# An encoder block on one core: output projection as seven products of halves, block sums by adding transfers, convolution norm inside attention, rows turned once

## The chip, the cores and the metric

The kernel runs on one core of one Trainium2 chip. The time is in device microseconds (us), one launch of the whole block. The engines of a core are TensorE (PE), VectorE (DVE), ScalarE (ACT), GpSimd (POOL) and SyncE (SP, which here only issues transfers); 16 DMA engines move data. Three runs of the kernel before gave 1063.12 to 1064.12 us, median 1063.84.

## The reference

One layer with 1024 tokens of width 1024, all in float32:

```python
h = rms_norm(x, norm1_g)
a, gate, q, k, v = jnp.split(h @ w_in, splits, axis=-1)
conv_out = conformer_conv(a, gate, dw_kernel, dw_bias, ln_g, ln_b)   # 512 channels
attn_out = neighbourhood_attention(norm(q), norm(k), v, rpb)         # 8 heads of 64
mix = jnp.concatenate([conv_out, attn_out], axis=-1)
x = x + mix @ w_out                                  # 1024 x 1024
h = rms_norm(x, norm2_g)
x = x + (silu(h @ w_gate) * (h @ w_up)) @ w_down     # width 2816
```

The convolution runs over positions with 31 taps per channel, then a LayerNorm over the 512 channels and a swish. Attention is over windows of 8 x 16 on a grid of 16 rows and 64 columns.

## The kernel before, in words

The whole block is one program in an order written out by hand; each engine works its list from front to back, and waits are put in where data or a buffer is needed. Matrix products use a split: each float32 operand is cut into a high part (a copy by ACT) and a low part (a subtraction by DVE or POOL), function `split`, lines 103 to 108, and one product becomes three matmuls, high x high, high x low, low x high (`mac`, lines 110 to 114). A matmul is 128x512. `weave` (line 119) puts a piece of other work between two groups of three matmuls.

Buffers come from pools with fixed counts: 22 tiles `G` of 128x1024, 6 tiles `H` of 128x4096, 3 raw tiles `R` for loads. In PSUM there are four banks `mm`, two `tp`, and a double one `cv`. Weights come through a list of loads (`want`); `take` (line 144) splits the next one and issues a load further ahead, so a load waits until the raw tile is free that an earlier split has read.

In order of time:

- Input projections: tiles of q, k, v (`nat`) and the gated convolution input (`glu_step`), with the convolution taps beside them on DVE (line 319), and some on ACT and POOL (lines 344, 345), summed into `u` at line 324.
- Attention (the loop at line 789), 32 pieces of two heads: `score_mm` (line 615), scores plus bias and exponential (lines 628, 630), normalisation on POOL (line 637), six transposes (line 646) with their copies (line 651), and the product with the values (line 662). Every fourth piece an output block is copied and split (lines 669, 674).
- Convolution norm after attention: the 512 channels of each of eight token tiles are turned to rows (line 728), statistics (lines 735, 736), root on ACT, scaling (lines 752, 756), then turned back and passed through the swish (lines 761, 762, 764).
- Output projection (`proj`, line 720): for each of eight token tiles and two halves of the columns, eight slices of the inner dimension, three matmuls each. Results are added to x from PSUM (`resid`, line 775). Weights `wo` are split by POOL.
- `norm2` (line 856) stores x for later, squares and sums on ACT; `norm2_out` (line 863) scales rows.
- FFN up: gate and up projections together as 2x2 blocks, in seven products per block i of 128 columns (m1 to m7, `product`, line 1013; `evac`, line 1024), 22 blocks. The weight operands are raw blocks or sums of them (`t_sums`, line 886, on DVE), split by `prep` (line 902). The token operands are A11, A12 (lines 991 to 995: four token tiles turned per slice) and S1, S2, S3, S4, A22, sums of halves of the normalised rows (`s_sum`, line 936), which `s_T` (line 950) turns and splits one after the other while the first products run.
- FFN down: seven products again (`down`, line 1211).

Of the kernel before, what the change touches and what calls it, by code (L numbers as in the profile page):

```python
# [7 lines left out]
F32R = mybir.dt.float32r  # L8
AF = mybir.ActivationFunctionType
# [3 lines left out]
P = 128  # L13
# [17 lines left out]
def layout(v):  # L31
# [4 lines left out]
    gu = np.stack([f["w_gate"], f["w_up"]]).reshape(2, KB, P, FB, P).transpose(3, 0, 2, 1, 4)  # L36
    wd = f["w_down"].reshape(FB, P, D)
# [14 lines left out]
        "wo": f["w_out"],  # L52
# [15 lines left out]
def build(ctx, tc, a):  # L68
# [22 lines left out]
    def SM(name, n=8):  # L91
        return T("sm", [P, 8], 16, name)[:, :n]

# [62 lines left out]
    def take_parts(jobs, n=4, sub=pool):  # L156
        i = pos[1]
        hi, lo = chunks[i][2]()
        w = 1024 // n

        def part(o):
            sl = slice(o, o + w)
            split(hi[:, sl], lo[:, sl], raws[i][:, sl], (sub,))
            if o + w == 1024:
                raws.pop(i)
                issue()
        pos[1] += 1
        jobs.extend(lambda o=o: part(o) for o in range(0, 1024, w))
# [18 lines left out]
    wo, woq = {}, {}  # L187

    def wo_dst(d, k0):
        def dst():  # L190
            if (d, k0 // 4) not in woq:
                woq[d, k0 // 4] = H(f"wo{d}{k0}", F32R)
            q = woq[d, k0 // 4]
            o = k0 % 4 * 1024
            hl = (q[:, o:o + 1024], q[:, o + 1024:o + 2048])
            for j in range(2):
                wo[d, k0 + j] = [w[:, j * 512:(j + 1) * 512] for w in hl]
            return hl
        return dst

    for d in range(2):
        for k0 in (4, 6, 0, 2):
            want(a["wo"][k0 * P:(k0 + 2) * P, d * 512:(d + 1) * 512].rearrange("(k p) m -> p k m", p=P),
                 f"wo{d}{k0}", wo_dst(d, k0), (pool,) * 4 if d == 0 and k0 < 4 else (pool,))
# [361 lines left out]
    for c in range(1, 4):  # L566
        for h in range(2):
            accs = {}
            for part in range(2):
                glu_step(c, h, part, accs)  # L570
                if c < 3 and part == 0 or c == 3 and (h, part) != (1, 1):
                    take(2 if c == 3 and h == part == 0 else 1)
    for t in range(8):
        project(0, t, head_post)
        if t % 2 == 0:
            take()
# [87 lines left out]

    def evac_hi(s_):
        rh, cb = order[s_]
        if rh == 0:
            at[cb] = [G(f"at{cb}{w}", F32R).rearrange("p (c t q) -> p c t q", c=4, t=2) for w in range(2)]
        act.copy(at[cb][0][:, :, rh], os_[s_])

    def evac_lo(s_, cs=slice(0, 4)):
        rh, cb = order[s_]
        hi, lo = [w[:, cs, rh] for w in at[cb]]
        dve.tensor_tensor(lo, os_[s_][:, cs], hi.bitcast(F32), OP.subtract)

    def value(t):
        z = nat(2, t)
# [35 lines left out]
    cm, x2, xn = [], {}, {}  # L713

    def lhs(k, t):
        if k < 4:
            return [w[:, k, t * P:(t + 1) * P] for w in cm]
        return [w[:, k - 4, t // 4, :] for w in at[t % 4]]

    def proj(t, d, acc, ks):  # L720
        for k in ks:
            mac(acc, lhs(k, t), wo[d, k], k == 4, k == 3)
            weave()

    def conv_T(t):
        y = cv(f"y{t}")[:, :512] if t in (0, 3) else tp(f"y{t}")
# [4 lines left out]
    cs = {}  # L731

    def conv_stats(t, y):
        st6, mv, sd = SM(f"bs{t}", 6), SM(f"bm{t}", 2), SM(f"bd{t}", 1)
        dve.bn_stats(st6, y)
        dve.bn_aggr(mv, st6)
        act.activation(sd, mv[:, 1:2], AF.Sqrt, bias=eps)
        cs[t] = y, mv, sd
        if 1 <= t <= 4:
            conv_scale(t - 1)  # L740
        if t >= 4:
            conv_scale(t)

    def conv_scale(t):
        y, mv, sd = cs.pop(t)
        r = SM(f"br{t}", 1)
        dve.reciprocal(r, sd)
        if t % 2 == 0:
            xx = G(f"xh{t}")
            xh.extend([xx[:, :512], xx[:, 512:]])  # L750
        if t >= 6:
            dve.tensor_scalar(xh[t], y, mv[:, 0:1], r, op0=OP.subtract, op1=OP.mult)
        else:
            nb = SM(f"bb{t}", 1)
            dve.scalar_tensor_tensor(nb, mv[:, 0:1], -1.0, r, OP.mult, OP.mult)
            act.activation(xh[t], y, AF.Identity, bias=nb, scale=r)

    def conv_silu(h, c):
        y = tp(f"z{h}{c}")
# [3 lines left out]
        hi, lo = [w[:, c, h * 512:(h + 1) * 512].rearrange("p (b i j) -> p i b j", b=4, j=16) for w in cm]  # L763
        split(hi, lo, y.rearrange("p (i b j) -> p i b j", b=4, j=16), (dve,))
# [9 lines left out]
    def resid(t, d, acc):  # L774
        dve.tensor_tensor(x2[t][:, d * 512:(d + 1) * 512], acc, x2[t][:, d * 512:(d + 1) * 512], OP.add)

    acc0, xh = [], []

    def attn_half(t):
        acc0.append(mm(f"pj{t}"))  # L780
        proj(t, 0, acc0[t], range(4, 8))

    def fill(*ks):
        if not acc0:
            act.activation(warm, eps, AF.Sqrt)
            acc0.append(mm("pj0"))
        proj(0, 0, acc0[0], ks)

    for i in range(2, 32 + 2):
# [6 lines left out]
        if i in (14, 22):  # L796
            take_parts(jobs)
        if i < 32:
            ss = score_mm(i)
        if i >= 32:  # L800
            fill(*((4, 5) if i == 32 else (6,)))
# [6 lines left out]
        flip_out(i - 2, 0)  # L808
        if i > 2:
# [3 lines left out]
            elif i > 6 and i % 4 in (0, 3):  # L813
                evac_lo((i + 1) // 4 - 2, slice(0, 2) if i % 4 == 3 else slice(2, 4))
        if jobs and i % 4 < 2:
            jobs.pop(0)()
    fill(7)

    cm += [H(f"cm{w}", F32R).rearrange("p (k s) -> p k s", s=S) for w in range(2)]
    conv_stats(0, conv_T(0))  # L820
    woven.extend([lambda: (weigh(31), evac_hi(7), evac_lo(7)), lambda: conv_stats(1, conv_T(1)), lambda: None])
    for t in range(2, 8):
        woven.extend([lambda t=t: conv_stats(t, conv_T(t)), lambda: None])
    take()
    attn_half(1)
    take()
    attn_half(2)
    attn_half(3)
    cc = cv("pj45")
    acc0 += [cc[:, :512], cc[:, 512:]]  # L830
    proj(4, 0, acc0[4], range(4, 8))
    act.activation(warm, eps, AF.Silu)
    conv_silu(0, 0)
    proj(5, 0, acc0[5], range(4, 8))
    for t in range(6):
        load_x2(t)
    later = [(0, c) for c in range(1, 4)] + [(1, c) for c in range(4)]
    woven.extend(lambda q=q: conv_silu(*q) for q in later)
    for ts in (range(4), (4, 5)):
        for k in range(4):  # L840
            for t in ts:
                mac(acc0[t], lhs(k, t), wo[0, k], False, k == 3)
                if t % 2:
                    weave()
        for t in ts:
            resid(t, 0, acc0[t])
    for t in range(6, 8):
        load_x2(t)
        acc0.append(mm(f"pj{t}"))
        proj(t, 0, acc0[t], (4, 5, 6, 7, 0, 1, 2, 3))  # L850
        take(2)
        resid(t, 0, acc0[t])
# [15 lines left out]

    HK, QF = KB // 2, FB // 2
    raw_gu, top, tsum = {}, {}, {}

    def load_gu(i, j):
        if i < FB:
            raw_gu[i, j] = R(f"gu{i}{j}")  # L880
            nc.sync.dma_start(raw_gu[i, j], a["gu"][ms[i], j])

    def lr(w):
        return w[:, :512], w[:, 512:]

    def t_sums(i, ns):
        (b11, b21), (b12, b22) = lr(raw_gu[i, 0]), lr(raw_gu[i, 1])
        for n in ns:
            if n in (1, 3):
                tsum[i, n // 2] = G(f"ts{i}{n}")  # L890
            o = lr(tsum[i, (n - 1) // 2])[(n - 1) % 2]
            l, r = ((b12, b11), (b22, lr(tsum[i, 0])[0]), (b22, b12), (b21, lr(tsum[i, 0])[1]))[n - 1]
            dve.tensor_tensor(o, l, r, OP.subtract)  # L893
# [3 lines left out]
    ms = [m + h * QF for m in range(QF) for h in range(2)]  # L897
    products = [(i, p) for p in ("m1", "m2", "m6", "m5", "m7", "m4", "m3") for i in range(2)]
    products += [(i, p) for i in range(2, FB) for p in ORDER]
    tasks = list(products)  # L900

    def prep(n=1):
        for _ in range(n):
# [3 lines left out]
            if i < 2:  # L907
                if i == 1 and p in ("m6", "m5"):
                    t_sums(i, (1, 2) if p == "m6" else (3, 4))
            elif p == "m1":  # L910
                t_sums(i, (1, 2))
            elif p == "m6":
                t_sums(i, (3, 4))
            b = {"m1": (0, 0), "m2": (0, 1), "m3": (1, 1)}.get(p)
            n = {"m5": 0, "m6": 1, "m7": 2, "m4": 3}.get(p)
            src = lr(raw_gu[i, b[0]])[b[1]] if b else lr(tsum[i, n // 2])[n % 2]
            top[i, p] = lr(G(f"t{i}{p}", F32R))
            split(*top[i, p], src, (dve,) if i < 2 and p in ("m1", "m2", "m6", "m5") else (pool,))
            if (i, p) == (0, "m2"):
                load_gu(1, 1)  # L920
            if (i, p) == (1, "m5"):
                load_gu(2, 0)
            if (i, p) == (0, "m3"):
# [330 lines left out]
```

## Time and profile before

| | |
|---|---|
| median of three runs | 1063.84 us |
| profiled execution | 1064.03 us, span 1062.2 us |
| instructions | 13969 |
| DVE busy | 699.8 us (66%) |
| ACT busy | 443.7 us (42%) |
| POOL busy | 397.3 us (37%) |
| moved by DMA | 144.05 MB, mean 136 GB/s |
| granted PE clock | 0.999 |

The span is the time from the first to the last instruction of one profiled execution; the rest of its own time lies around it. Busy time of an engine is the sum of its instructions. A group row reads: line, engine, operation, what is written <- what is read, shape, count | busy time, mean ns of one | idle time of the engine before them and what ended it. L112 is line 112. A chain row reads: start, length, what ran. PEld is the weight load of PE, which runs beside the matmuls.

### The profile page before, as it was taken

What the parts mean: (1) busy time and instruction counts of PE and PEld (TensorE: products, weight loads), DVE (VectorE), ACT (ScalarE), POOL (GpSimd) and SP (SyncE); (2) the same over time, 40 slices, a digit from 0 to 9 for tenths busy, and PEclk for the clock granted to TensorE, in tenths of its full rate; (3) what the DMA queues carried; (4) which work ended last, traced back from release to release, by engine and by line L of the source; (5) the groups of instructions that cost most, each with busy time, mean ns of one, the idle gap of its engine ahead of it and who ended that gap; (6) DMA issues with size and microseconds to landing.
All of it is one profiled execution on the core that took longest, in us unless ns stands there. A gap on an engine that the chain in (4) does not pass through costs nothing.

```text
span 1062.2 us, 13969 instructions
## 1 busy us (share of the span) xinstructions
PE 1045.4 (98%) x5068; PEld 847.3 (80%) x5068; DVE 699.8 (66%) x1072; ACT 443.7 (42%) x874; POOL 397.3 (37%) x308
## 2 busy tenths in 40 slices
PE   7999999999999999999999999999999999999997
PEld 5788888776667888788888888888888888888886
DVE  6768998966765247666565564564655567858883
ACT  6456346626776334532323223332233344433441
POOL 0126568823542301444554544545454200002310
PEclk9999999999999999999999999999999999999999
DMA  9416681245504412032322222232132597634641
GB/s 333 164 47 225 217 257 36 75 161 154 165 34 161 136 80 99 21 129 77 136 91 104 109 99 95 104 129 100 70 131 78 194 322 276 209 99 132 205 127 43
DMA packets 68244, 144.05 MB, mean 136 GB/s; under 512 B 12496, under 2 KB 21200, under 8 KB 67536
## 3 DMA queue, kind: packets, MB, share of 16 engines
q1 hardware_dynamic: 66336, 139.95, 38.3%
q10 hardware_dynamic: 1840, 3.22, 0.9%
q8 instruction: 40, 0.66, 0.3%
q14 instruction: 28, 0.23, 0.1%
HBM read 103.99 MB, written 44.76 MB: 140 GB/s over the span
## 4 chain that ended last, share of the span: by engine, by line
PE 94%; DMA 2%; DVE 1%; ACT 1%; POOL 1%; issue 0%; SPq 0%; POOLq 0%; ACTq 0%
PE B L112 6%; PE B L114 6%; PE B L113 6%; PE A L112 4%; PE D L112 4%; PE D L114 4%; PE A L114 4%; PE D L113 4%; PE A L113 4%; PE z L113 3%; PE z L112 3%; PE z L114 3%; PE gl L114 3%; PE gl L112 3%; PE gl L113 3%; PE o L662 2%
## 5 line engine op out<-in xcount | busy, mean ns | idle before, releaser
L319 DVE SCALAR_TENSOR_TENSOR cv<-u,par,cv 128x1009 f32<-128x1009 f32 (+14 forms) x85 | 108.5, 1276 | 1.9
L345 POOL TENSOR_TENSOR pa<-pa,pr 128x1022 f32<-128x1022 f32 (+10 forms) x31 | 74.2, 2392 | 35.5 <-ACT pr L344 26.5
L104 ACT CAST op<-sr 128x512 fp32r<-128x512 f32 x77 | 47.7, 619 | 52.1 <-PE B2d L114 26.3
L108 DVE TENSOR_TENSOR op<-sr,op 128x512 fp32r<-128x512 f32 x77 | 57.1, 742 | 16.1 <-ACT op L104 16.0
L1037 DVE TENSOR_TENSOR g<-B,g 128x512 f32<-128x512 f32 x22 | 15.2, 691 | 79.0 <-PE B L114 79.0
L1209 POOL TENSOR_TENSOR ou<-ou,resm 128x512 f32<-128x512 f32 x8 | 12.2, 1530 | 144.0 <-DMA resm<-xd 142.1
L1046 ACT ACTIVATE D<-D 128x512 f32<-128x512 f32 x22 | 12.8, 582 | 113.1 <-DVE D L1045 113.1
L1032 DVE TENSOR_TENSOR u<-B,g 128x512 f32<-128x512 f32 x22 | 15.2, 691 | 62.1 <-PE B L114 62.1
L104 ACT CAST op<-wd 128x512 fp32r<-128x512 f32 x66 | 40.9, 620 | 30.7 <-DVE wd L1124 18.4
L637 POOL TENSOR_SCALAR e<-e,rs 128x288 f32<-128x288 f32 (+1 forms) x64 | 34.1, 545 | 50.2 <-DVE rs L635 42.9
L108 DVE TENSOR_TENSOR op<-wd,op 128x512 fp32r<-128x512 f32 x66 | 50.4, 764 | 1.8
L893 DVE TENSOR_TENSOR ts<-gu,ts 128x512 f32<-128x512 f32 x44 | 51.0, 1159 | 0.8
L1035 ACT ACTIVATE A<-A 128x512 f32<-128x512 f32 x20 | 11.6, 582 | 76.3 <-PE A L114 76.3
L630 ACT ACTIVATE e<-e,mx 128x288 f32<-128x288 f32 (+1 forms) x64 | 36.2, 569 | 2.0 <-DVE mx L628 2.0
L628 DVE CUSTOM_DVE_ANT_0 e<-s,tab 128x288 f32<-128x288 f32 (+1 forms) x64 | 30.1, 505 | 8.1 <-PE s L615 8.0
L344 ACT ACTIVATE pr<-u,par 128x1022 f32<-128x1022 f32 (+10 forms) x31 | 34.2, 1135 | 1.2 <-ACT vs L405 1.2
L893 DVE TENSOR_TENSOR ts<-gu 128x512 f32<-128x512 f32 x22 | 34.1, 1551 | 0.0
L646 PEld LDWEIGHTS p<-ident,e 128*96 128x96 f32 (+1 forms) x192 | 20.1, 133 | 15.2 <-issue 10.5
L944 POOL TENSOR_TENSOR xn<-xn,xn 128x512 f32<-128x512 f32 x4 | 6.9, 1732 | 57.3 <-DVE sn L944 57.3
L646 PE MATMUL p<-ident,e 128*96 128x128 f32 (+1 forms) x192 | 27.6, 280 | 0.7 <-DVE pT L651 0.6
L662 PE MATMUL o<-pT,vw 96*64 96x128 f32 (+1 forms) x384 | 28.0, 281 | 0.0
L615 PE MATMUL s<-kT,qT 64*128 64x288 f32 (+1 forms) x128 | 26.7, 495 | 0.0
(1039 smaller groups left out, 3449.6 us busy)
## 6 DMA issues: line engine op xcount, KB each, us to landing
gu<-in_gu SPq DMA_DIRECT2D x44, 512.0 KB
sr<-sd SPq DMA_DIRECT2D x77, 256.0 KB
sd<-sd SPq DMA_DIRECT2D x22, 512.0 KB
wd<-in_wd SPq DMA_DIRECT2D x44, 256.0 KB
sd<-g SPq DMA_DIRECT2D x33, 256.0 KB
x<-in_x SPq DMA_DIRECT2D x16, 512.0 KB
xd<-x SPq DMA_DIRECT2D x8, 512.0 KB
resm<-xd SPq DMA_DIRECT2D x16, 256.0 KB
```

Source lines behind the costliest of these rows:

```text
L104: act.copy(hi, src)
L108: eng.tensor_tensor(*[w[..., sl] for w in (lo, src, hi.bitcast(F32))], OP.subtract)
L112: pe.matmul(acc, lh, rh, start=start, stop=False, skip_group_check=True)
L113: pe.matmul(acc, lh, rl, start=False, stop=False, skip_group_check=True)
L114: pe.matmul(acc, ll, rh, start=False, stop=stop, skip_group_check=True)
L319: dve.scalar_tensor_tensor(acc[:, o], uc[:, i], dwk[:, c, t:t + 1], acc[:, o], OP.mult, OP.add)
L344: act.activation(pr[:, o], uc[:, i], AF.Copy, scale=dwk[:, c, t:t + 1])
L345: pool.tensor_tensor(pa[:, o], pa[:, o], pr[:, o], OP.add)
L630: act.activation(e[:, hh], e[:, hh], AF.Exp, bias=mx, scale=-1.0, accum_out=rs[:, hh:hh + 1])
L646: pe.transpose(pt[:m, g * P:(g + 1) * P], es[i][:, hh, g * m:(g + 1) * m], ident)
L662: pe.matmul(os_[s_][hh * HD:(hh + 1) * HD, hp], vw[cb, rh + g][:, c:c + HD], pTs[i][:, g, hh], start=g == 0, stop=g == 2)
L893: dve.tensor_tensor(o, l, r, OP.subtract)
```

## The change

- **Output projection in seven products.** Tokens are taken in two halves (the first and the second 512), mix columns as attention and convolution, weights as four blocks B11 to B22. Products n1 to n7 use the left operands a11, Q3, A22, Q2, Q1, A12, Q4 and the right ones B11, P3, P4, P2, P1, B21, B22. Each product is four token blocks of four slices; its result is added to or subtracted from one or two quarters of x (`read`, `put`), and n7 and n5 are accumulated on the banks of n1 and n6. The left sums are built on DVE as the attention blocks and convolution slices come (`evac_lo`, `conv_diff`) and split by POOL (`q_split`).
- **Block sums by transfers.** P1 to P4 are made in DRAM: SyncE copies one block, POOL issues a transfer that adds another. For the projection each of the four sums is done in two parts, in the q and v projections and in attention (`aside_sum`); for the first four blocks of the FFN weights in one part each, between the seven groups of the projection (`gate_sum`). Those blocks' operands are then loaded ready-made and split by POOL; the products of the first four blocks are put in another order.
- **Convolution norm inside attention.** `conv_norm` turns a tile in every third piece (eight in all), takes its statistics and copies it to SBUF. The inverse roots of all eight tiles are then worked out on DVE, by an integer estimate and three steps, and the tiles scaled on DVE two at a time, in pieces 25 to 31.
- **Rows turned once.** Each normalised row tile is turned as a whole by `turn` (8 transposes, two PSUM tiles), copied to SBUF, and S1 to S4 and A22 are summed and split there; before, every operand was turned by itself.

```diff
+    def sum_steps(w, parts):
+        h = P // parts
+        def put_(n, m, i):
+            return lambda: nc.sync.dma_start(pw[w, n][i * h:i * h + h], block(w, m)[i * h:i * h + h])
+        def add(n, m, i):
+            return lambda: pool.dma_start(pw[w, n][i * h:i * h + h], block(w, m)[i * h:i * h + h], accum_op=OP.add,
+                                          max_dma_last_dim=2048)
+        return [f(n, m, i) for n, l, r in (("P3", "B12", "B22"), ("P1", "B12", "B11"), ("P2", "P1", "B22"),
+                                           ("P4", "P2", "B21"))
+                for f, m in ((put_, l), (add, r)) for i in range(parts)]
...
+    steps = sum_steps("w4", 2)
+    late_steps = sum_steps("g4", 1)
...
     for t in range(8):
         project(0, t, head_post)
+        if t in (1, 3):
+            aside_sum()
...
     def value(t):
+        if t % 2:
+            aside_sum()
...
+            hi, lo = [w[:, cs] for w in a11[cb]]
+            dve.tensor_tensor(lo, os_[s_][:, cs], hi.bitcast(F32), OP.subtract)
+            dve.tensor_tensor(diff[j][:, :, cb], os_[s_][:, cs], rowf[j][:, :, cb], OP.subtract)
...
+    def conv_norm(t):
+        y = conv_T(t)
+        st6 = SM(f"bs{t}", 6)
         dve.bn_stats(st6, y)
+        dve.bn_aggr(mvs[:, t], st6)
...
+        act.copy(xh[t], y)
...
+    def conv_scale(t, eng):
+        eng.tensor_scalar(xh[t], xh[t], mvs[:, t, 0:1], rc[:, t:t + 1], op0=OP.subtract, op1=OP.mult)
...
+        if i in (13, 17, 21, 25):
+            take_parts(jobs, more=i < 21)
+        if i % 3 == 0:
+            aside_sum()
+        if i in (32, 33):
+            issue()
...
+        if i % 3 == 0 and i < 27:
+            conv_norm(i // 3 - 1)
+        if i == 25:
+            root = rsqrt(rc, mvs[:, :, 1], "rc")
+        if 25 <= i < 28:
+            next(root)
+        if 28 <= i < 32:
+            conv_scale(2 * i - 56, dve)
+            conv_scale(2 * i - 55, dve)
...
+    def turn(t, j):
...
+        pt = (tp, mm)[j](f"t2{t}{j}")
+        for i in range(4):
+            kb = 4 * j + i
+            pe.transpose(pt[:, i * P:(i + 1) * P], xn[t][:, kb * P:(kb + 1) * P], ident)
...
+    weaves(16, s1=C(0, 2), s5=take, s9=C(0, 3), s13=QS("Q2", diff, 0, pool))
+    group("n7")
+    gate_sum(2)
+    weaves(16, s0=C(1, 0), s2=QS("Q2", diff, 1, pool), s4=take, s6=C(1, 1), s9=take, s12=QS("Q1", rowf, 0, pool))
+    group("n4")
+    gate_sum()
+    weaves(16, s0=C(1, 2), s2=take, s5=C(1, 3), s7=QS("Q1", rowf, 1, pool), s10=take, s13=QS("Q4", diff, 0, pool))
+    group("n6")
+    gate_sum()
+    weaves(16, s1=take, s3=QS("Q4", diff, 1, pool), s6=take, s9=N(0), s13=N(3))
+    group("n5")
+    gate_sum()
...
+    weaves(16, s0=take, s1=[N(1), U(0, 0)], s2=U(0, 1), s3=[lo2, lo2], s4=U(3, 0), s5=[U(3, 1), N(2)], s6=[lo2, lo2],
+           s7=U(1, 0), s8=U(1, 1), s9=[lo2, lo2, prep], s10=[U(2, 0), take], s11=U(2, 1), s12=[lo2, lo2], s13=prep)
+    group("n2")
+    gate_sum()
+    weaves(16, s3=prep, s7=prep, s9=N(4), s12=U(4, 0), s13=[U(4, 1), N(7)], s15=SS(0, 1, 2))
+    group("n3")
...
+    plan = {
+        0: dict(s0=U(7, 0), s1=[U(7, 1), N(5)], s2=SP("S2", 0), s3=SS(3, 1, 2)),
+        1: dict(s0=U(5, 0), s1=[U(5, 1), N(6)], s2=SP("S2", 3), s3=SS(1, 1, 2)),
+        2: dict(s0=U(6, 0), s1=[U(6, 1), lambda: act.activation(warm, eps, AF.Silu)], s2=SP("S2", 1), s3=SS(2, 1, 2)),
+        3: dict(s0=SP("S2", 2), s2=SP("S1", 0), s3=SP("S1", 3)),
...
+        13: dict(s1=SP("A22", 2), s3=SP("A22", 3)),
+    }
...
+    products = [(i, p) for k in (0, 2) for p in ("m1", "m2") for i in (k, k + 1)]
+    products += [(i, p) for k in (0, 2) for p in SRC for i in (k, k + 1)]
+    products += [(i, p) for i in range(4, FB) for p in ORDER]
```

In the weaves, s0 to s15 are the places after each three matmuls of a group; C is a slice of the convolution's swish, N the scaling of a row tile, U half a turn, SS sums and SP a split of the token operands, QS a split of a left operand of the projection. Before n1 and before n7 four tiles of x each are loaded, and two sum steps (`gate_sum(2)`) come ahead of n7 too.

More of the change, by code (lines that the diff above doesn't have):

```diff
@@ L8 @@
 F32R = mybir.dt.float32r
+I32 = mybir.dt.int32
 AF = mybir.ActivationFunctionType
@@ L165, in part @@
                 raws.pop(i)
-                issue()
+                if more:
+                    issue()
         pos[1] += 1
@@ new lines, in N, with U, SS, SP @@
+    def N(t):
+        return lambda: norm2_out(t)
+    def U(t, j):
+        return lambda: turn(t, j)
+    def SS(t, *ns, eng=dve):
+        return lambda: s_sum(t, ns, eng)
+    def SP(n, t, eng=dve):
+        return lambda: s_split(n, t, eng)
+    lo2 = lambda: rest.pop(0)()
+    def group(p, cbs=CB):
+        for cb in cbs:
+            more = p in ("n7", "n5")
+            if not more:
+                pb[cb] = mm(f"{p}{cb}")
+            proj(p, cb, pb[cb], start=not more)
+            read(p, cb)
```

471 lines of the change are left out of this document (256 added, 215 removed).

## The prediction, made before the result was known

> **What bounds the kernel now.** I read the first part of the page, then the busy time by stage, then what TensorE (PE) waited for, then the chain of waits in order of time.
>
> ```profile
> span 1062.2 us, 13969 instructions
> PE 1045.4 (98%) x5068; PEld 847.3 (80%) x5068; DVE 699.8 (66%) x1072; ACT 443.7 (42%) x874; POOL 397.3 (37%) x308
> ```
> ```profile
> 0.00:31.00 31.00, 24.09 (x95) 19.43 (x96) 19.14 (x46) 18.55 (x39) 0.68 (x6) 1.00 0.94 344
> 240.00:312.00 72.00, 71.30 (x652) 46.54 (x651) 53.03 (x192) 53.94 (x165) 36.61 (x66) 1.00 0.42 130
> 358.00:421.00 63.00, 62.44 (x291) 51.58 (x291) 31.43 (x49) 18.68 (x35) 9.03 (x5) 1.00 0.30 109
> 421.00:470.00 49.00, 48.46 (x249) 39.21 (x248) 34.49 (x48) 25.37 (x43) 21.53 (x17) 1.00 0.19 70
> 470.00:930.00 460.00, 460.00 (x2032) 380.87 (x2031) 275.14 (x358) 147.58 (x267) 183.85 (x136) 1.00 0.38 137
> ```
> ```profile
> PE z L112 <- ACT wk0h L104: 6.9, 1, 6.9
> PE t L994 <- DVE xn L867: 0.6, 1, 0.6
> ```
>
> Columns of the stage rows: start and end, length, busy time of PE, its weight loads, DVE, ACT, POOL, then granted clock, DMA share, GB/s. PE is busy in every stage at full clock; its only long wait is 6.9 us at the start, the next relevant one 0.6. So PE's instruction list sets the time: an instruction fewer is time saved, wherever the other four engines and the DMAs keep up. The attention stage (240 to 312) is the one that bears watching: DVE and ACT are both three quarters busy there.
>
> A busy PE is not yet the price of a matmul, because ends overlap (389 ns is recorded for one). The price is the distance of starts, from the chain:
>
> ```profile
> 79.30 0.44 PE zt L392 x4
> 85.23 0.44 PE zt L392 x4
> 324.42 0.44 PE y L728 x4
> 326.25 0.44 PE y L728 x4
> ```
>
> The first pair is one projection tile: 24 matmuls and 4 transposes in 5.93 us. The second is 6 matmuls and 4 transposes in 1.83. The difference, 18 matmuls in 4.10, gives 0.228 us for a matmul of 128x512 and 0.46 for four transposes.
>
> **What PE loses.**
>
> ```profile
> L112 PE MATMUL pj<-wo,at 128*128 128x512 f32 x32 | 13.7, 429 | 0.0
> L113 PE MATMUL pk<-wo,cm 128*128 128x512 f32 x32 | 12.5, 389 | 0.0
> L994 PE MATMUL t<-ident,xn 128*128 128x128 f32 x32 | 5.0, 274 | 0.6 <-DVE xn L867 0.6
> L963 PE MATMUL sq<-ident,xn 128*128 128x128 f32 x24 | 3.6, 272 | 0.0
> L963 PE MATMUL sp<-ident,sn 128*128 128x128 f32 x16 | 2.1, 272 | 0.0
> ```
>
> The output projection is twelve such groups of 32 (first and last shown), 384 matmuls. Seven products of halves are 7 x 4 token blocks x 4 slices x 3 = 336: 48 fewer, 48 x 0.228 = 10.9 us. Transposes for the FFN are 32 (line 994) and 80 (four groups of line 963, 24+24+16+16, first and last shown); each row tile turned once needs 64: 48 fewer, 12 fours x 0.46 = 5.5. The 32 of the convolution norm and the 32 before its activation stay, the former only move into attention. PE: **-16.4 us**. The FFN from its fifth block on keeps its products; its sums are still on DVE.
>
> **Attention (adds).** 30 iterations fill 240 to 312, 2.4 us each, DVE 53.03 / 30 = 1.77, ACT 1.80, POOL 1.22.
>
> ```profile
> L735 DVE BATCH_NORM_STATS2 bs<-y 128x6 f32<-128x512 f32 x8 | 5.6, 695 | 2.4 <-PE y L728 2.4
> L736 DVE BATCH_NORM_AGGREGATE bm<-bs 128x2 f32<-128x6 f32 x8 | 1.5, 182 | 0.3
> L674 DVE TENSOR_TENSOR at<-o,at 128x256 fp32r<-128x256 f32 x13 | 5.4, 412 | 0.0
> L635 DVE RECIPROCAL rs<-rs 128x2 f32<-128x2 f32 x29 | 4.8, 166 | 12.6 <-ACT e L630 12.6
> L755 DVE SCALAR_TENSOR_TENSOR bb<-bm,br 128x1 f32<-128x1 f32 x6 | 1.8, 304 | 0.4 <-DVE br L747 0.2
> L752 DVE TENSOR_SCALAR xh<-y,bm,br 128x512 f32<-128x512 f32 x2 | 1.6, 810 | 0.1
> ```
>
> In the eight iterations with a convolution tile DVE gets 0.88 more and PE 0.46: 2.65 against 2.86, it fits. The end does not: in iterations 25 to 31 DVE has 7 x 1.59 (53.03 less the 5.4 of line 674, over 30) = 11.1, the four pieces of lo and difference 1.6, the 13 small steps of the inverse root at 0.166 (0.304 at most) 2.2, and eight scalings of 128x512. No row has that scaling from SBUF. The nearest is line 752, the same operation from PSUM, 0.81; the other end is an instruction with hardly any data, 0.30. I take 0.7, nearer to the first: 5.6. Sum 20.5 in 7 x 2.4 = 16.8, less the 0.6 by which DVE runs ahead in one iteration: **+3.0 us** (0 to 5). The Trainium skill (VectorE: DVE Perf Modes, Mode 2×_2P) says that a single-source operation with source and destination in SBUF passes two elements a cycle; by that, an estimate of 0.35 each, this term would be about 0.2 and the time 1051. No row of this trace has such an operation, so the sum stays with line 752.
>
> POOL gets eight more quarter splits and six adding transfers inside the loop. Their issue on POOL has no row; SyncE's issues take 0.6 median, 10 at worst when its queue is full:
>
> ```profile
> L600 SPq DMA_DIRECT2D vw<-vd x16: 507/608/10160, 217.5 to 276.6; - x16
> 208.97 7.29 POOL L345 TENSOR_TENSOR pa<-pa,pr 128x1014 f32<-128x1014 f32 x3 [0.52 <-ACT pr L344]
> 228.15 1.22 DVE L324 TENSOR_TENSOR u<-cv,pa 128x1024 f32<-128x1024 f32 x1
> ```
>
> At about 1 us they hide in POOL's 1.2 spare per iteration. The two ahead of attention hide in the 11.9 us between POOL's last tap (216.26) and DVE's use of it (228.15). The sums P1, P2, P4 follow each other three to six iterations apart (7 to 15 us), more than 0.5 MB needs, so SyncE's copies behind them should not stand; where one does, the loads of P3 and P4 queue behind it, and those are due 12 us later. Cost 0, up to 2 if an issue takes 2 us.
>
> **Projection (adds).** Each group is 48 matmuls, 10.9 us.
>
> ```profile
> L775 DVE TENSOR_TENSOR x<-pk,x 128x512 f32<-128x512 f32 x8 | 5.5, 687 | 6.0 <-PE pk L114 6.0
> L108 POOL TENSOR_TENSOR wo<-wo10r,wo 128x1024 fp32r<-128x1024 f32 x1 | 2.4, 2402 | 0.0
> L104 ACT CAST h<-t 128x512 fp32r<-128x512 f32 x8 | 4.5, 584 | 3.6 <-PE t L994 3.6
> ```
>
> DVE has 40 additions instead of 16: 24 x 0.687 = 16.5 more, plus 12 differences of 0.69, beside PE. n1 is its fullest group: eight additions 5.5, the last attention block 1.6, five steps of the convolution 3.5, 10.6 against 8.7 of PE, and the first of these differences waits for POOL's split of Q3. What is late there are banks that PE needs again a group later: cost 0. POOL is tighter. In n4 it has the second half of Q2, two halves of P2 and one of Q1, 4 x 2.4 = 9.6, behind an adding transfer that must wait until the copy of 1 MB before it has landed; n6 has 9.6 too. Ahead of that copy go P4 (1 MB), x (4), P2 (1), the first copy and its sum (2 to 4), itself 1: 9 to 11 MB, at the 344 GB/s of the first stage row 26 to 32 us. From P4's load, some 5 us before n1, to the start of n4 are 5 + 8.7 + 11.8 = 25.5. So it lands 0.5 to 6.5 us into n4, P2 is split 8.2 later (issue 1, three splits), and n6 needs it at 11.8 + 1.4: a stall of 0 to 1.5. On SyncE the copy of P2 waits for P1's sum, and behind it stand the loads that POOL splits a group later. In n2 ACT copies 16 half tiles, 16 x 0.584, and some 3.3 of weight splits: 12.6 of 14.6 (10.9 and eight fours). I take **+2.0** for the stage (0 to 10, the upper end by the third rival). The Trainium skill (DMA: Bandwidth & Descriptors, Anatomy of one DMA) gives about 2 us plus bytes / 436 GB/s; by that, an estimate of 4.4 us for 1 MB, copy and sum each end 1.4 us later than at 344 GB/s and n6's stall rises to about 3. No run here shows an adding transfer.
>
> **First FFN products (adds).** Operands are split from SBUF where they came from PSUM. The last row tile's norm, its turn and its split follow within two products of 2.74 us; behind DVE's share of 3.4 per product I expect PE to stand about 1 us at the last turn. S2 is due eight products (22 us) later. **+1.4** (0 to 5).
>
> **Sum.** -16.4 + 3.0 + 2.0 + 1.4 = -10.0; span 1052.2. The profiled execution took 1064.03, 1.8 beyond its span, and lies 0.2 above the median of 1063.84: 1052.2 + 1.8 - 0.2 = 1053.8, say **1054**.
>
> **Rivals.** *A: all cover holds.* The three additions are 0, and the 1.1 us that PE idled in the stage rows 358 to 470 goes too: 1046 to 1047. For it: leads of a group or more. Against: DVE's sum in the last iterations.
>
> *B: DVE falls behind in the first products.* Its subtractions now read both inputs from SBUF while POOL splits weights.
>
> ```profile
> L893 DVE TENSOR_TENSOR ts<-gu 128x512 f32<-128x512 f32 x22 | 34.1, 1551 | 0.0
> L1120 DVE TENSOR_TENSOR wd<-wd 128x512 f32<-128x512 f32 x11 | 7.5, 686 | 0.8 <-DMA wd<-in_wd 0.7
> ```
>
> The same kind of work took 1.55 us beside a working POOL and 0.69 without. Over 14 products (38 us) DVE has 32 such steps (20 splits, 12 sums), 22 us, and 12 of evacuation and norm. If half of them meet POOL, 16 x 0.86 = 14 more: 48 us, when A22 is due after 16 products, 44. PE waits some 4 to 5 us: 1058 to 1059. The Trainium skill (SBUF — State Buffer, Who interferes with whom) has this as a rule: two SBUF inputs on DVE contend with a POOL instruction that reads SBUF; these two rows agree.
>
> *C, slower: the adding transfers are slow and POOL stands.* If a sum moves at a third of the plain rate and a copy inside DRAM at half, 13 to 16 MB stand ahead of P1's copy, 38 to 46 us against 25.5; P2 is split 8.2 later, 7.5 to 16 us after n6 needs it, and the next sums, one behind the other, add a few more. At 18 us: 1062.2 - 16.4 + 3.0 + 1.4 + 18 + 1.6 = 1070. It decides from 12 us of standing on. For it: no row shows such a transfer and POOL cannot work past one. Against: the sums have a group each.
>
> **How the numbers follow.** My sum 0.50, A 0.12, B 0.17, C (with milder forms of it near no change) 0.21. A measurement of this kernel can tell 0.2%, 2.1 us. Faster: the first three, 0.79, less 0.02 for a B that goes further: 0.77. C splits into 0.05 within the bound and 0.16 beyond, so 0.07 same, 0.16 slower. The range goes from A's end, 1046, to 1068, which leaves out the worse half of C.
>
> **What would show it.** PE's count falls by 96 (48 of line 112's kind, 48 transposes) and PE's distances stay 0.228. The last iterations of attention come out longer than 2.4 us with DVE as releaser; no PE wait on POOL before n6. Wrong it would be if PE waits on POOL's splits for over 10 us in all (C), on DVE's S or A22 operands (B), or if the iterations with a convolution tile are longer by more than 0.5.

## The result and the profile after

The changed kernel took 1088.32 us (median of 4 runs, 1088.18 to 1088.57), the kernel before, on the same chip, 1063.98 (1063.12 to 1064.22): a ratio of 1.023, 95% interval 1.0213 to 1.0248. It is 24 us slower, where 10 us less were forecast.

The page of the changed kernel, its span, the first engines' line and the slices of PE's granted clock:

```profile
span 1086.4 us, 13896 instructions
PE 1036.1 (95%) x4972; PEld 838.0 (77%) x4972; DVE 722.5 (67%) x1097; ACT 464.0 (43%) x911; POOL 453.9 (42%) x342
PEclk9999999999789899999999999999999999999999
```

PE has 96 instructions fewer, as forecast, and is busy 9 us less although its clock fell in three slices; yet the span is 24 us longer. The time is nearly all idle time, and most of it lies in two places. A *flip* below is the six transposes of one attention piece (`p<-ident,e`). Starts of PE's work in the timeline, before / after: first flip to last flip of attention 74.4 / 103.3 us; from there to the first FFN product 100.7 / 99.9; from there to the first product of the down projection 429.8 / 426.8; from there to the end of PE's last product 209.9 / 209.9. The waits of the changed kernel from 240 to 420 us (waiter <- awaited: total, times, longest):

```profile
POOL g4P L212 <- DMA g4P<-in_g: 19.7, 1, 19.7
PE p L682 <- POOL e L673: 17.4, 4, 12.1
POOL w4P L212 <- DMA w4P<-w4P: 15.9, 2, 11.7
PE n L123 <- POOL wP L118: 10.8, 1, 10.8
```

PE waited 17.4 us for the norm of the scores on POOL (line 673), 12.1 and 4.3 of it in two stalls, and 10.8 us for a weight split on POOL (line 118). The split is that of P4's second half, which product n4 needs (tile n; the kernel runs n1, n7, n4, n6, n5, n2, n3, and the section on the change lists the operands in that order). In the two long stalls and before that split POOL was not working: it stood at an adding transfer (line 212) until the copy before it had landed. POOL's timeline has the places (start, duration, and in brackets the idle time before):

```profile
284.37 0.91 POOL L212 DMA_DIRECT2D w4P<-in_w  x1 [11.67 <-DMA w4P<-w4P]
299.29 0.91 POOL L212 DMA_DIRECT2D w4P<-in_w  x1 [4.24 <-DMA w4P<-w4P]
376.73 1.04 POOL L212 DMA_DIRECT2D g4P<-in_g  x1 [19.68 <-DMA g4P<-in_g]
```

The issue of an adding transfer costs POOL about 1 us, as estimated. Why the copies landed late is on SyncE's timeline of the changed kernel:

```profile
247.47 18.48 SPq L636 DMA_DIRECT2D vw<-vd  x4
266.05 2.34 SPq L624 DMA_DIRECT2D tab<-tf  x1
268.48 0.55 SPq L209 DMA_DIRECT2D w4P<-w4P  x1
269.12 14.33 SPq L636 DMA_DIRECT2D vw<-vd  x4
283.55 2.53 SPq L209 DMA_DIRECT2D w4P<-w4P  x1
354.63 2.39 SPq L209 DMA_DIRECT2D g4P<-in_g  x1
```

A *ring* is the queue of transfers that one engine has issued and that are not done. Four loads of value windows hold SyncE for 18.5 us, then 14.3. The copy of 0.5 MB issued between them at 268.48 has landed at 284.37, 15.9 us later; the next, issued at 283.55, at 299.29; the 1 MB of line 209 at 354.63 by 376.73, 22 us later. The busy share of the 16 DMA engines and the rate, in 40 slices from 247 to 265 us of the changed kernel:

```profile
DMA  2397999999999989999999999984232123222213
GB/s 100 125 284 264 332 314 309 269 314 314 253 257 282 337 237 282 346 282 337 323 300 346 337 196 250 269 221 143 100 152 107 82 102 143 109 109 109 109 82 146
```

There are two levels: a share of 0.9 and about 300 GB/s while the table (128 rows) is loaded, and 0.2 and about 105 GB/s while only value windows are. A window's source is 4 grid rows of 24 or 32 columns; 4 of 16 engines would be a share of 0.25 (the view gives the mean of the 16, not which of them worked). The x loads of the projection (8 grid rows of 16 columns) run at 0.4 to 0.5 and about 200 GB/s in most slices, here from 354 to 377 us:

```profile
DMA  4545549974467999948445545554578933158763
```

The Trainium skill has a rule for this (DMA: Bandwidth & Descriptors, Why a DMA increments its semaphore by 16 and not by 1): the number of engines is the largest one up to 16 that divides the slowest dimension of both sides. By it a window gets 4 and an x block 8; both levels agree. The level was there to be read before the change, in the same stretch of the kernel before:

```profile
DMA  2269799999999899999799953322222222122222
```

So the theory after the result has two parts. SyncE is held at window and x loads, so the copies behind them are issued late; and a transfer spread over all 16 engines that is queued in SyncE's ring behind loads on 4 or 8 of them is complete only when its share on those few has come through; POOL stands at the dependent sum, PE behind POOL. Its rivals: the copies are slow for their own bytes or for the adding transfers' (the forecast's case C), or ring order alone does it, whatever the number of engines.

PE also lost clock. Stages of the changed kernel (start:end, length, busy PE, PEld, DVE, ACT, POOL, granted clock, DMA share, GB/s):

```profile
268.00:273.00 5.00, 5.00 (x50) 3.54 (x50) 3.41 (x14) 4.53 (x17) 2.65 (x5) 1.00 0.90 247
273.00:278.00 5.00, 0.81 (x4) 0.19 (x4) 0.71 (x3) 1.23 (x4) 0.00 (x0) 1.00 0.74 233
278.00:280.00 2.00, 0.00 (x0) 0.00 (x0) 0.00 (x0) 0.00 (x0) 0.00 (x0) 0.52 0.25 105
280.00:285.00 5.00, 0.00 (x0) 0.00 (x0) 0.00 (x0) 0.00 (x0) 0.63 (x1) 0.50 0.25 104
285.00:290.00 5.00, 4.11 (x22) 2.69 (x22) 1.68 (x6) 2.07 (x6) 3.11 (x7) 0.50 0.98 249
290.00:295.00 5.00, 4.85 (x36) 3.14 (x36) 2.00 (x7) 2.45 (x7) 2.35 (x4) 0.83 0.99 302
```

PE stops at 273.8 us; from about 278 the granted clock is a half, and the work after the stall (285 to 290) still runs at it.

### The profile page after: what moved, and what is told of

It reads as the page before. It is cut to its first block, busy times and chain, and to the rows that moved or that the text cites. A ratio compares the mean times of both kernels' runs of the same rounds, so it can differ in the third digit from the quotient of the medians.

```text
span 1086.4 us, 13896 instructions
## 1 busy us (share of the span) xinstructions
PE 1036.1 (95%) x4972; PEld 838.0 (77%) x4972; DVE 722.5 (67%) x1097; ACT 464.0 (43%) x911; POOL 453.9 (42%) x342
## 4 chain that ended last, share of the span: by engine, by line
PE 83%; issue 5%; POOL 3%; DVE 3%; DMA 2%; ACT 2%; SPq 0%; POOLq 0%; DVEq 0%; ACTq 0%
PE B L122 5%; PE B L124 5%; PE B L123 5%; PE z L122 4%; PE z L123 4%; PE D L124 4%; PE D L123 4%; PE D L122 4%; PE z L124 4%; PE A L124 3%; PE A L123 3%; PE A L122 3%; PE gl L124 3%; PE gl L122 3%; PE gl L123 3%
## 5 line engine op out<-in xcount | busy, mean ns | idle before, releaser
L114 ACT CAST op<-wd 128x512 fp32r<-128x512 f32 x66 | 40.9, 620 | 31.9 <-DVE wd L1281 17.2
L682 PE MATMUL p<-ident,e 128*96 128x128 f32 (+1 forms) x192 | 30.0, 294 | 20.3 <-POOL e L673 17.4
L984 DVE TENSOR_TENSOR ts<-ts,gu 128x512 f32<-128x512 f32 x36 | 43.3, 1203 | 0.6
L870 DVE TENSOR_TENSOR x<-x,n 128x512 f32<-128x512 f32 x40 | 26.2, 682 | 19.1 <-PE n L124 12.7
L687 ACT COPY pT<-p 96x384 f32<-96x384 f32 (+1 forms) x32 | 15.3, 477 | 37.0 <-PE p L682 34.1
L984 DVE TENSOR_TENSOR ts<-gu 128x512 f32<-128x512 f32 x18 | 30.0, 1666 | 0.0
(1057 smaller groups left out, 3529.3 us busy)
```

Source lines behind the costliest of these rows:

```text
L114: act.copy(hi, src)
L682: pe.transpose(pt[:m, g * P:(g + 1) * P], es[i][:, hh, g * m:(g + 1) * m], ident)
L984: dve.tensor_tensor(lr(tsum[i, 1])[n - 3] if o is None else o, l, r, OP.add)
```

## The experiments

The kernel before took 1063.4 to 1063.6 us beside each group of runs. "Stretches" below are first to last flip of attention, then last flip to first FFN product; in the kernel before they are 74.4 and 100.7, in the changed kernel 103.3 and 99.9.

**1. No sums for the output projection.** Raw blocks stand where the sums P1 to P4 of w_out belong, so those products use wrong weights; no copies or adding transfers of that set.

```
-        return a[w][BLK[n]] if n in BLK else pw[w, n]
+        n = RAWB.get(n, n) if w == "w4" else n
-    steps = sum_steps("w4", 2)
+    steps = []
```

> Leaves out the sums P1 to P4 of the output projection's weights (copies and adding transfers in q, v and attention); the raw blocks stand in for them, so the output differs. All else is the changed kernel. My theory (POOL stands at the adding transfers of P2 in attention until SyncE's copies have landed): the stretch from the first to the last flip of attention, 103.3 us in the changed kernel and 74.8 before, comes down to 79 to 82 (74.8 + 3.7 for the convolution's transposes + up to 3), the time to 1062 to 1068. Rival 1 (the convolution norm fills DVE and ACT in attention): the stretch stays above 92, the time above 1077.

Measured 1067.65 us, ratio 1.0031 (1.0016 to 1.0045). Stretches 88.3 and 94.9. The stall of 12 us is gone, one of 3.9 us at 295 stays without any sum in attention, and 5.2 us in n4. The time fits the theory's range, the attention stretch doesn't (79 to 82 was expected): the sums of the output projection are behind some 20 us, 15.0 of them in attention and 5.0 after it, and something else also stops attention at 295.

**2. No sums for the FFN blocks.** As in 1, for the set of the gate and up weights.

```
-            late_steps.pop(0)()
+            pass
```

> Leaves out the sums of the first four FFN blocks' weights (four copies and four adding transfers of 1 MB in the projection); raw blocks stand in, so the output differs. My theory (POOL stands for 20 us at the first of them, and the split of P4 behind it makes PE wait 10.8 us and lose its clock): the stretch from the last flip to the first FFN matmul, 99.9 us, comes down by 11 to 14, the time to 1074 to 1077. Rival (POOL's own splits, 9.6 us in a group of 10.9, are the bound of the projection): the stretch falls by less than 4, the time stays above 1084.

Measured 1076.25 us, ratio 1.0121 (1.0099 to 1.0144); stretches 106.0 and 85.7, no gap over 0.3 us in the projection. The stall there belongs to the FFN sums alone; without it the projection is 15.0 us shorter than before the change (2.9 of them are the convolution's transposes, which moved into attention).

**3. Copies from ScalarE.** All twelve copies (eight halves for w_out, four for the FFN) are issued by ACT, so they stand in its ring; nothing left out.

```
-            return lambda: nc.sync.dma_start(pw[w, n][...], block(w, m)[...])
+            return lambda: nc.scalar.dma_start(pw[w, n][...], block(w, m)[...])
```

> All copies of the sums (16 in all: eight and eight halves counted as in the change) are issued by ACT instead of SyncE, at the same places of the program; same bytes, same adding transfers. My theory (the copies are late because they stand in SyncE's ring behind loads that use 4 or 8 of the 16 DMA engines): on a ring of their own they land in some 4 to 8 us; both stalls nearly go, 1052 to 1064. Rival 2 (copies inside DRAM or adding transfers are slow in themselves, or the DMA engines are full): the time stays above 1080, since bytes and engines are the same.

Measured 1088.19 us, ratio 1.0225 (1.0199 to 1.0251): a miss. The waits of POOL in this run for the copies of w_out are gone, but others took their place:

```profile
DVE x L870 <- DMA x<-in_x: 15.2, 5, 6.5
PE p L682 <- POOL e L673: 9.8, 4, 8.2
ACT wP L114 <- DMA P30r<-w4P: 8.5, 1, 8.5
```

The raw load of P3 is in SyncE's ring too, and ACT's split of it stands at the head of ACT's queue, with the flips behind it. In the projection DVE waits for x; one x load landed 31.8 us after its issue. Why is not shown: in run 4, with no copy left in the projection, one also took 31.9. The price moved from POOL's queue to ACT's and DVE's.

**4. Copies before attention.** All twelve copies are issued in the q projection (P2 and P4 start from raw blocks, so that no copy waits for a sum); only the sums stay. Nothing left out.

```
-                                           ("P2", "P1", "B22"), ("P4", "P2", "B21"))
+                                           ("P2", "B22", "P1"), ("P4", "B21", "P2"))
...
-        if t in (1, 3):
-            aside_sum()
+        if t < 4:
+            for _ in range(3):
+                copies.pop(0)()
```

> All twelve copies are made in the q projection, when the DMA engines are nearly idle; P2 and P4 start as copies of B22 and B21 and the earlier sum is added to them, so no copy waits for a sum. The adding transfers stay on POOL, those of P2 and P4 at pieces 3, 6, 12 and 15 of attention, the FFN's at n7, n4, n5 and n3. Nothing is left out. My theory: no adding transfer finds its copy missing, the two stalls go, 1047 to 1056. Rival 2 (adding transfers slow in themselves): POOL still stands, now at the sum before, above 1075. Rival 1 (convolution norm): above 1070.

Measured 1068.19 us, ratio 1.0048 (1.0029 to 1.0068); stretches 94.0 and 92.9. POOL waits for no copy any more: 20 us are back. What is left is one stall of 9.2 us at 295, and two of 3.3 together in the projection, for x. The chain of waits of this run (start, length, what) and the row of its waits name it:

```profile
283.30 19.21 DMA P30r<-w4P
```
```profile
ACT wP L114 <- DMA P30r<-w4P: 9.4, 1, 9.4
```

It is P3's load, 19.2 us from issue to landing for 0.5 MB. The kernel before split two chunks in attention, both loaded ahead of it; the change splits four and loads two inside.

**5. The same, with P3's two loads from ScalarE.**

```
-            take_parts(jobs, more=i < 21)
+            take_parts(jobs, more=False)
+        if i in (18, 22):
+            issue(nc.scalar)
```

> The kernel of the run with all copies before attention, with one more edit: the two raw loads of P3 that are issued inside attention go out from ScalarE's queue instead of SyncE's. Nothing is left out. Theory (ring order): P3's load landed 19.2 us after its issue only because it stood in SyncE's ring behind value-window loads that use 4 of the 16 DMA engines; on another ring it lands within 4 to 8 us, the 9.15 us stall of TensorE at 295 us goes with the clock that it cost, and the time is 1055 to 1058 (1068.2 less 9.15 less 1 to 3). Rival (the DMA engines as a whole are short of time there, in whatever ring the load stands): the load still lands 12 us or more after its issue, 1064 to 1069.

Measured 1058.72 us, ratio 0.9955 (0.9941 to 0.997): 0.45% faster than the kernel before, and within a microsecond of the expectation. Nobody waits for P3; stretches 86.8 and 87.2. One stall of 2.6 us remains at 289, DVE at a table load that took 20.7 us in the same ring.

**6. And x from contiguous rows.** The host lays out a copy of x in the order of the windows; nothing left out.

```
-        nc.sync.dma_start(x2[t], rows(a["x"], t))
+        nc.sync.dma_start(x2[t], a["xw"][t * P:(t + 1) * P])
```

> The run before this one, and the eight loads of x for the residual read 128 contiguous rows each from a copy of x that the host lays out in the order of the windows, instead of eight grid rows of 16 columns; nothing is left out. Theory (a source of 8 rows is served by 8 of the 16 DMA engines): the loads take half as long, VectorE's waits for x at 365 and 369 us go (3.3 us of TensorE), and the time is 2 to 4 us under the run before it, 1051 to 1055. Rival (x is late because its loads are issued late, at 334.8 us): within 1 us of the run before it.

Measured 1058.84 us, ratio 0.9961 (0.9945 to 0.9977): no difference to run 5. Run 5 had no wait for x left that this edit could remove; the rival's number was right, though not for its reason.

**7. And no scaling of the convolution's rows** (their norm is not applied).

```
-            conv_scale(2 * i - 56, dve)
-            conv_scale(2 * i - 55, dve)
+            pass
```

> The run before this one without the eight scalings of the convolution's rows at pieces 28 to 31 (mean and variance are still taken; the rows stay unscaled, so the convolution's part of the output is not normed). If the scalings on VectorE are what holds TensorE at pieces 28 to 31, the gaps of 1.00 and 0.56 us there and the one before go and the time falls by 1.5 to 3 us. Rival (the gaps are the statistics', the root's or the mask adds' own): within 0.6 us of the run before it.

Measured 1058.06 us, ratio 0.995 (0.9933 to 0.9966). The attention stretch is 2.5 us shorter (84.4 against 86.9; 0.5 of it is the wait for a table) and one of the last two gaps is gone, the other (1.0 us) is not. The median moves by 0.8 only, within the intervals; in the profiled executions 0.8 is given back behind the first FFN product, for a reason that was not followed. The tile view of the changed kernel has the scaling's price:

```profile
L832 DVE TENSOR_SCALAR xh<-xh,par x8: 535/538/541, 331.7 to 340.0; 128x512 f32<-128x512 f32 x8
```

**8. The changed kernel with contiguous windows and x.** Copies and sums stay where they are. Each window load reads as many contiguous rows of the value scratch (other rows, so attention weighs wrong values), x as in 6.

```
-        nc.sync.dma_start(vw[cb, g], vd.rearrange("(r c) d -> r c d", c=GW)[g * 4:g * 4 + 4, c0:c0 + ncol, :])
+        nc.sync.dma_start(vw[cb, g], vd[g * 4 * GW:g * 4 * GW + 4 * ncol, :])
```

> The changed kernel itself, copies and adding transfers where they are, with two edits: every value-window load reads as many contiguous rows of the value scratch instead of 4 grid rows of 24 or 32 columns (the same bytes to the same place, but other rows, so attention weighs wrong values), and x is read from contiguous rows as in the run before. Theory (it is the few DMA engines of those loads that make SyncE's ring slow, not its order or its bytes): the copies of 0.5 MB land within 6 us of issue instead of 15.8, the stalls of 12.1 and 4.3 us in attention go to under 3 together, the FFN copy of 1 MB behind the x loads lands within 12 us instead of 22 and the stall of 10.8 us falls to 0 to 4; 1055 to 1064. Rival (the ring's order and bytes alone): 1083 to 1089.

Measured 1057.12 us, ratio 0.9942 (0.9927 to 0.9957). The same bytes in the same ring in the same order, only from one block of 96 or 128 rows in place of 4 strips (x: 128 in place of 8): 31.2 us less than the changed kernel. SyncE's timeline of this run, and one of POOL's sums:

```profile
241.63 2.97 SPq L637 DMA_DIRECT2D vw<-vd  x4
254.08 0.53 SPq L210 DMA_DIRECT2D w4P<-w4P  x1
261.13 1.75 SPq L637 DMA_DIRECT2D vw<-vd  x4
```
```profile
281.72 0.91 POOL L213 DMA_DIRECT2D w4P<-in_w  x1
```

Four window loads hold SyncE for 3.0 and 1.8 us instead of 18.5 and 14.3, and no sum of w_out finds POOL waiting (the row shown has no bracket, nor have the others). The copy that the changed kernel issued at 268.48 goes out at 254.08 here, 14.4 us earlier. By these times the held issuer alone is more than the first stall of 11.7 us: issued at 254, a copy that took 15.9 us would still have landed before POOL came to its sum at 272.7. What each of the two parts costs was not tried apart. The first FFN copy lands 12.0 us after its issue, and POOL stands 5.2 us for it instead of 19.7. This decides against the rivals: bytes, order and adding transfers are those of the changed kernel.

**9. Contiguous windows alone.** The edit to vw of 8; wrong values again.

> The changed kernel with the one edit that the value-window loads read contiguous rows (same bytes, other rows, so attention weighs wrong values); x is read as before. With the run that had both edits at 1057.1 and the changed kernel at 1088.3, 31.2 us are to be shared out. Theory: the windows are behind the two stalls in attention and the clock lost in them, the x loads behind the stall of 10.8 us in the projection. So the attention stretch is 83 to 85 us as in the run with both edits, a stall of 7 to 12 us at the fourth product stays, and the time is 1065 to 1070. Rival (the copy of the FFN block is late only because attention ran late): no stall over 3 us in the projection, 1057 to 1061.

Measured 1068.41 us, ratio 1.0043 (1.0027 to 1.0058). Attention 83.7; the projection's stall stays, 10.1 us:

```profile
POOL g4P L212 <- DMA g4P<-in_g: 19.8, 1, 19.8
```

**10. Contiguous x alone.** The edit of 6 in the changed kernel.

> The changed kernel with the one edit that x for the residual is read from contiguous rows (a copy of x laid out by the host in window order; nothing is left out); the windows are loaded as before. Theory: attention stalls as in the changed kernel, 102 to 104 us from first to last flip, and the projection's stall of 10.8 us falls to 0 to 4, so 1074 to 1080. Rival (the FFN copy is slow for its own bytes or behind what attention left in the ring): 1085 to 1089.

Measured 1077.89 us, ratio 1.0136 (1.0122 to 1.015). Attention 105.1, about as in the changed kernel, the projection 88.3 with no stall over 1.2 us. The FFN copy lands 11.9 us after its issue (SyncE's row, then POOL's) instead of 22.

```profile
352.35 0.51 SPq L210 DMA_DIRECT2D g4P<-in_g  x1
364.24 1.04 POOL L213 DMA_DIRECT2D g4P<-in_g  x1 [4.97 <-DMA g4P<-in_g]
```

The windows cost 19.9 us, x 10.4, together 30.3 of the 31.2: two separate groups of stalls with one kind of cause.

**11. A way to get such windows without wrong values.** Run 6, with ACT storing each value tile in eight pieces, one for each of two grid rows and four windows, so that a window is contiguous in memory.

```
-        nc.scalar.dma_start(vd[t * P:(t + 1) * P, :], vs)
+        for cb in (0, 3, 1, 2):
+            c0, ncol, _ = WIN[cb]
+            for r in range(2):
+                nc.scalar.dma_start(vd[cb][(2 * t + r) * ncol:...], vs[r * GW + c0:r * GW + c0 + ncol, :])
```

> The run with copies before attention, P3's loads from ScalarE and contiguous x, with one more edit that leaves nothing out: ScalarE stores each value tile as eight pieces, one for each of two grid rows and four windows, so that a window's load reads contiguous rows. Theory: the wait of 2.9 us at 288.8 us (VectorE for a table that stands in SyncE's ring behind window loads) goes and little is added, since ScalarE is busy for a third of the value stage: 1054 to 1057. Rival (56 more stores of 48 to 64 KB hold ScalarE or make the first windows late): 1058 to 1063.

Measured 1074.03 us, ratio 1.0097 (1.0083 to 1.0111): a miss by 17 us. ACT's timeline of this run, in the value stage:

```profile
223.74 7.94 ACTq L433 DMA_DIRECT2D vd<-vs  x8
231.78 0.69 ACT L429 ACTIVATE vs<-z,r 128x512 f32<-128x512 f32 x1 [8.59 <-DMA vd<-vs]
```

Eight small stores hold ACT for 7.9 us, and the next tile's evacuation waits for them; PE stood 5.2 us there and 7 us in the first pieces of attention. That ACT was two thirds free did not help: the issues themselves held it. Whether by the length of its ring or by the number of DMA engines that each store got was not tried apart.

**12. And the scalings spread.** One each at pieces 28 to 31, two each at 32 and 33.

```
-        if 28 <= i < 32:
-            conv_scale(2 * i - 56, dve)
-            conv_scale(2 * i - 55, dve)
+        for t in {32: (4, 5), 33: (6, 7)}.get(i, (i - 28,) if i >= 28 else ()):
+            conv_scale(t, dve)
```

> The run before this one with the eight scalings of the convolution's rows one each at pieces 28 to 31 and two each at 32 and 33, where no scores are taken, instead of two each at 28 to 31. Nothing is left out. If it is VectorE's room in pieces 28 to 31 that makes the gaps of 1.0 and 0.55 us there, 0.8 to 1.6 us less than the run before. Rival (the scalings at 32 and 33 delay the first convolution steps of the projection by as much): within 0.5 us of it.

Measured 1073.21 us, ratio 1.0096 (1.0082 to 1.011). The gap of 0.56 us at piece 30 is gone, the one of 1.0 stays; 0.8 less in the median, the same ratio. Not worth a claim.

## Why the prediction was wrong

**The step that failed** is the one for copies and loads: "so SyncE's copies behind them should not stand" in attention, priced 0 to 2, and the sum "9 to 11 MB, at the 344 GB/s of the first stage row" in the projection, priced 0 to 1.5. The first gave no rate at all; the second counted the x loads ahead of the copy, but at the rate of a row from the start of the kernel, where the 16 DMA engines were 0.94 busy. Neither asked how fast the loads already in SyncE's ring would run. In attention the ring ran at about 105 GB/s while windows were in it, in the projection at about 200 with x. In place of 0 came stalls of 12.1 and 4.3 us, in place of 1.5 one of 10.8; with the clock lost that is the 31.2 us that run 8 gives back. The place was off too: the sum let POOL stand at the second adding transfer, P1's, and PE at n6; POOL stood at the first, P3's, ahead of n7, and PE at n4, whose weight split came behind it. The row of line 600 (median issue 0.6 us, worst 10.16) was read only for the price of an issue on POOL, which came out right at about 1 us. It also held the warning: an issuer is at times held by what is already in its ring, in this stretch of the changed kernel 18.5 us for four issues. For that the prediction had no term.

**Rival C** had the sign and the wait (POOL standing at the sums, PE after it), but not the mechanism, and its 1070 was too low by 18. It priced slow adding transfers and copies. The page of the changed kernel has them (issue to landing):

```profile
w4P<-in_w POOLq DMA_DIRECT2D x8, 512.0 KB, 6.1
g4P<-in_g POOLq DMA_DIRECT2D x4, 1024.0 KB, 10.2
```

That is about 85 to 105 GB/s, nearly the "third of the plain rate" that C supposed, and run 8 is fast with the same sums in it. Its place was off too: two thirds of the loss is in attention, which C priced at 3.0, and the rest at n4, not at n6. The prediction's own sign against itself did come: PE waited 10.8 us on POOL's splits, over the 10 that it named.

**What held.** PE: 96 instructions fewer. Between the kernel before and run 8, from the distances of starts, the output projection's matmuls after the last flip take 88.9 and 76.9 us, 12.0 less where 10.9 was forecast; the stretch from first FFN product to down projection is 3.0 shorter with 3.3 more idle, so 6.3 less work where 5.5 was; the convolution's and row blocks' transposes ahead of it took 2.4 more than before, forecast as nothing. Together 15.9 against 16.4.

*Attention's DVE term* was +3.0. In run 8, where no sum of w_out waits for its copy, the attention stretch is 9.2 us longer than before, 4.2 of it the transposes that moved in; the other 5.0 are 3.6 of idle time and 1.4 of longer distances. Three gaps at its end make 2.6, the first of them behind POOL:

```profile
309.21 1.10 PE L683 MATMUL p<-ident,e 128*128 128x128 f32 x6 [0.92 <-POOL e L674]
313.12 0.85 PE L683 MATMUL p<-ident,e 128*128 128x128 f32 x6 [1.15 <-DVE pT L688]
316.17 0.84 PE L683 MATMUL p<-ident,e 128*128 128x128 f32 x6 [0.56 <-DVE pT L688]
```

The scaling in it was priced 0.7 from a PSUM row, with an estimate of 0.35 by the Trainium skill (VectorE: DVE Perf Modes, Mode 2×_2P); it took 0.538, between them. With 0.538 the prediction's sum gives 1.8, and run 7, without the scalings, took 2.0 off the stretch beside the table wait. So this mechanism is there at about its price; the rest of the 5.0 is spread over the later pieces and was not followed.

*Projection*, +2.0: in run 8 PE idles 2.5 us more there than before, 1.2 at a turn and 1.6 at a weight split on POOL, with no wait for x.

*First FFN products*, +1.4, took 3.3: 1.2 at the turn of a row tile, as named, but another 2.7 at the first products of the next group, which was not foreseen (0.4, 0.8, 1.1 and 0.4, alike in nearly every run), less the 0.5 that PE idled there before the change. B's long wait for S2 and A22 did not come.

*Clock.* The prediction had no term for it. The stalls of the changed kernel in attention and projection sum to 27.1; run 8 gives back 31.2. By the distances of starts from the first flip to the first FFN product, the changed kernel has 25.0 us more idle time than run 8, and the same instructions take 5.5 us longer; that fits PE's half clock after each stall (4.1 busy us at 0.50 from 285 to 290). The Trainium skill has the rule (TensorE: Matmul & The Clock Gate, Part 1: The HAM clock gate): the clock is a half after at least one idle window of about 3.4 us. The trace agrees: it fell some 4 us after PE stopped.

With the cause taken away (runs 5 and 8) the kernel takes 1057 to 1059, not 1054: PE's term stands, and attention and the first products cost some 2 us each more than forecast.

## What to carry to other kernels

Before a transfer is put into a queue, read what else stands in that queue and at what share of the DMA engines it runs: here a share of 0.2 to 0.25 in the slices stood for loads from 4 strips of rows, 0.4 to 0.5 for loads from 8, and what came behind them in the ring was late by those loads, not by its own bytes. A median issue time far below the worst one (0.6 and 10.16 us here) went with a ring that at times holds its issuer; and a wait on the queue of an engine that also works (POOL's sums, ACT's splits and stores) is a wait of the whole pipeline. If such a load can't be given another shape cheaply, issue the large transfers ahead of it or on another ring (run 5), and don't pay for the shape with many small stores (run 11).

## What was not expected of the hardware

A copy of 0.5 MB took 15.9 us and a load of 0.5 MB 19.2 us in a ring with loads from 4 strips of rows, against a median of 6.1 us for the adding transfers of the same size from POOL's own queue. PE's granted clock stood at 1.00 until 278 us, about 4 us after PE stopped at 273.8, then at 0.50; after the restart at 285.9 it needed about 6 us to come back. Eight stores of 48 to 64 KB held their issuer for 7.9 us.
